# A two-layer hybrid trunk on one core: background products paced by counted TensorE work, sparse values prepared apart, latent queries projected first

## The chip, the cores and the metric

The kernel runs on one core of a Trainium2 chip. The metric is the device time of one execution in microseconds, the median of several runs.

## What is computed

The reference is a decoder trunk of two layers, 512 tokens of width 1024, in float32. A layer normalises its input, projects it at once for four groups of four heads, lets each group attend causally, joins the outputs in one projection that is added to the input, and runs a squared-ReLU MLP of width 4096.

```python
h = rms_norm(x, norm1[l]); proj = h @ w_in[l]
qa = rms_norm(a_cq, mla_q_norm[l]) @ mla_w_uq[l]      # a: latent attention, last 32 of a query's 96 rotated
kv = rms_norm(a_ckv, mla_kv_norm[l]) @ mla_w_ukv[l]
o_a = causal_block_attention(q_a, k_a, kv[..., 64:], 96 ** -0.5)
o_b = sliding_window_attention(q_b, k_b, v_b, sinks[l], Dh ** -0.5)
o_c = dsa_attention(q_c, k_c, v_c, qi, ki, c_w, 128, Dh ** -0.5)   # each query keeps its 128 best keys
o_d = causal_block_attention(..., log_f_cum=cumsum(log_sigmoid(d_f + b)))
x = x + concat(o_a, o_b, o_c, o_d) @ w_out[l]
x = x + square(relu(rms_norm(x, norm2[l]) @ w_up[l])) @ w_down[l]
```

## The kernel before, in words

**Arithmetic.** Every float32 operand of a product is split into a high part (`hi`, a rounding copy, L123 to L127) and a low part (`lo`, the difference, L133 and L135), and a product is three matmuls (`mm3`, L138 to L140): high by high, low by high, high by low. Weights arrive by DMA in `raw` tiles of 512 KB; ScalarE writes the high part `wh`, VectorE or POOL the low part `wl`.

**Stages of a layer.** First comes the projection for the indexer and its scores. Then all other input projections stand in a queue of generators: a, b0, b, d0, d, dv, c0, c, cv, then the four parts o0 to o3 of the output projection over the six head pairs that are ready first. Each step of a generator is one background product, one `mm3` of 128 x 256 (L138 to L140 with `wh` and `T`). After the latent projections (a), the kernel turns them, projects keys and values and then queries from them (four token tiles each), and rotates the queries tile by tile with four operations on POOL (`rotate`, L461 to L466). `prep_a` transposes the rotated queries (L843), then splits them and issues single moves from SP (`move`, L481) that put high and low parts of two heads into stacked tiles `stk`.

**Attention units.** 64 units follow in `run_units`: 16 latent (a), 16 window (b), 16 forgetting (d), 16 sparse (c). A unit is one head's block of 128 queries: score (for d L948 to L950, for c L884 to L893), softmax (VectorE's maximum L538, ScalarE's exponential L541, VectorE's reciprocal L542, POOL's normalisation L546), two units later the transposes of the probabilities and their split (`p_parts`, L552), another two later the product with the values (L595 to L599, L1000 and L1003). Every eight units a new pair of heads begins; its preparation (`prep_b`, `prep_d`, `prep_c`) transposes its rows (`parts`, L487), splits them and moves them through SP. `FIRST` gives the unit from which a preparation may start and `LAG` how many units its projection must have been done. The sparse preparation needs both "c" (keys) and "cv" (values).

**What sets the order.** At each site of the program `fill(kind)` takes as many products from the queue as the next digit of that kind's string says: `u0`, `u1`, `u2` are the three sites of a unit. The selection of the sparse keys is done in 51 VectorE steps (L759 search, L760 replacement, L763) that `extra` issues after the units at the rate `selr`, one rate for each 16 units. An output part starts when a pair's `mixed` rows are four units old (`mlag`); its last products are added to the residual tile T by VectorE (L446). All SP issues stand in one in-order queue, weight loads (L217) and moves alike.

```python
            def fill(kind):
                n = Q.get(kind, "")
                j = site.get(kind, 0)
                site[kind] = j + 1
                for _ in range(int(n[j], 36) if j < len(n) else 0):
                    if not queue or not advance():
                        break
```

## Time and profile before

| | |
|---|---|
| median of 3 runs | 1339.31 us (1338.87 to 1339.56) |
| profiled execution, its own time | 1341.57 us |
| its span | 1339.8 us |
| mean granted TensorE clock | 0.983 |
| busy: TensorE, VectorE, ScalarE, POOL | 1266.1, 733.0, 568.3, 271.4 us |
| DMA | 136.79 MB, mean 102 GB/s |

A time is in microseconds from the start of the span. A line is that of the kernel before. Matmuls overlap: each shows about 0.28 us for 256 columns, though the next one starts earlier, so the time of a run of matmuls is the distance of their starts. The granted clock of 1.00 is 2.4 GHz, 0.5 is 1.2 GHz; a stretch shows its mean. Idle time of an engine is put down to what ended it, and "issue" means that nothing in the profile shows it. In layer 0 attention lies between about 100 and 305 us, in layer 1 between 760 and 965.

### The profile page before, as it was taken

How to read it: one execution, taken by the hardware profiler on the slowest of the kernel's cores; microseconds unless marked ns; L12 is line 12 of the kernel's file. 1: busy time of each engine (PE TensorE's matmuls, PEld its weight loads, DVE VectorE, ACT ScalarE, POOL GpSimd, SP SyncE). 2: the span in 40 equal slices, each digit the busy share in tenths (PEclk: the TensorE clock that was granted, in tenths of full speed). 3: DMA queues.
4: the chain of work that ended last, by engine and by line, in shares of the span. 5: the costliest groups of instructions: out<-in, count | busy, mean ns of one | idle time of the engine just before them, and what ended most of it. 6: DMA issues, size and time to landing. Idle time of an engine off the chain costs nothing.

```text
span 1339.8 us, 19388 instructions
## 1 busy us (share of the span) xinstructions
PE 1266.1 (95%) x7226; PEld 1106.7 (83%) x7232; DVE 733.0 (55%) x1523; ACT 568.3 (42%) x1159; POOL 271.4 (20%) x390
## 2 busy tenths in 40 slices
PE   8889989799999999999989899897999999999997
PEld 7779988698888888888888799887888888888885
DVE  4748989745453334433366498895454523344344
ACT  5745556643442113332337455574344411233231
POOL 3453346331000000000024632642400000000011
PEclk9989999899999999999999999998999999999998
DMA  5135426422333333334412443353333333333331
GB/s 179 48 105 156 106 77 158 102 78 74 110 95 94 98 104 94 97 95 126 138 61 73 118 122 107 91 139 80 105 93 95 95 95 99 96 103 96 110 111 63
DMA packets 50818, 136.79 MB, mean 102 GB/s; under 512 B 7460, under 2 KB 7716, under 8 KB 50724
## 3 DMA queue, kind: packets, MB, share of 16 engines
q1 hardware_dynamic: 50724, 135.55, 35.2%
q8 instruction: 57, 0.93, 0.3%
q14 instruction: 37, 0.30, 0.1%
HBM read 106.95 MB, written 4.19 MB: 83 GB/s over the span
## 4 chain that ended last, share of the span: by engine, by line
PE 79%; DVE 11%; ACT 3%; POOL 3%; issue 2%; DMA 1%; SPq 0%; POOLq 0%; ACTq 0%; DVEq 0%
PE bank L138 24%; PE bank L139 23%; PE bank L140 23%; PE bank L552 2%; DVE wl L133 1%; DVE m L759 1%; DVE mn L538 1%; DMA stk<-prt 1%; DVE isc L760 1%; DVE prt L133 1%; PE bank L597 1%; ACT y L125 1%; PE bank L248 1%; POOL y L465 1%; DVE pt1l L133 1%
## 5 line engine op out<-in xcount | busy, mean ns | idle before, releaser
L123 ACT ACTIVATE wh<-raw 128x1024 fp32r<-128x1024 f32 (+2 forms) x196 | 199.4, 1020 | 286.4 <-PE bank L139 246.5
L133 DVE TENSOR_TENSOR wl<-raw,wh 128x1024 fp32r<-128x1024 f32 (+2 forms) x154 | 188.8, 1228 | 229.6 <-ACT wh L123 229.2
L138 PE MATMUL bank<-wh,T 128*128 128x256 f32 (+3 forms) x864 | 272.6, 316 | 13.7 <-DVE T L446 8.4
L140 PE MATMUL bank<-wl,T 128*128 128x256 f32 (+3 forms) x864 | 257.9, 299 | 1.3 <-DVE wl L133 0.9
L139 PE MATMUL bank<-wh,T 128*128 128x256 f32 (+3 forms) x864 | 257.3, 298 | 0.2 <-DVE T L135 0.2
L140 PE MATMUL bank<-T,wh 128*128 128x512 f32 x512 | 199.5, 390 | 1.0 <-DVE T L135 1.0
L138 PE MATMUL bank<-T,wh 128*128 128x512 f32 x512 | 199.8, 390 | 0.0
L138 PE MATMUL bank<-wh,gh 128*128 128x512 f32 x512 | 199.6, 390 | 0.0
L139 PE MATMUL bank<-T,wl 128*128 128x512 f32 x512 | 199.5, 390 | 0.0
L140 PE MATMUL bank<-wl,gh 128*128 128x512 f32 x512 | 199.2, 389 | 0.0
L139 PE MATMUL bank<-wh,gl 128*128 128x512 f32 x512 | 199.2, 389 | 0.0
L138 PEld LDWEIGHTS bank<-wh,T 128*128 128x128 f32 x864 | 168.8, 195 | 18.7 <-DVE T L446 6.8
L133 POOL TENSOR_TENSOR wl<-raw,wh 128x1024 fp32r<-128x1024 f32 (+3 forms) x42 | 88.2, 2100 | 447.6 <-DVE wl L133 336.5
L140 PEld LDWEIGHTS bank<-wl,T 128*128 128x128 f32 x864 | 168.2, 195 | 4.3 <-DVE wl L133 1.8
L139 PEld LDWEIGHTS bank<-wh,T 128*128 128x128 f32 x864 | 168.9, 196 | 3.2 <-DVE T L135 0.5
L1111 DVE TENSOR_TENSOR a<-a 128x512 f32<-128x512 f32 x64 | 44.3, 693 | 154.1 <-ACT a L1110 154.1
L1110 ACT ACTIVATE a<-bank 128x512 f32<-128x512 f32 x64 | 38.3, 598 | 201.2 <-PE bank L140 201.2
L140 PEld LDWEIGHTS bank<-T,wh 128*128 128x128 f32 x512 | 96.1, 188 | 21.9 <-DVE T L135 1.8
L139 PEld LDWEIGHTS bank<-T,wl 128*128 128x128 f32 x512 | 96.1, 188 | 20.5 <-DVE wl L133 0.7
L138 PEld LDWEIGHTS bank<-T,wh 128*128 128x128 f32 x512 | 96.1, 188 | 20.0 <-ACT T L252 0.3
L138 PEld LDWEIGHTS bank<-wh,gh 128*128 128x128 f32 x512 | 96.1, 188 | 20.0
L546 POOL TENSOR_SCALAR pr<-pr,sm 128x256 f32<-128x256 f32 (+3 forms) x128 | 72.9, 570 | 195.9 <-DVE sm L542 166.9
(209 smaller groups left out, 1852.8 us busy)
## 6 DMA issues: line engine op xcount, KB each, us to landing
raw<-in_wu_dram SPq DMA_DIRECT2D x64, 512.0 KB, 3.6
raw<-in_wd_dram SPq DMA_DIRECT2D x64, 512.0 KB, 3.6
stk<-prt SPq DMA_DIRECT2D x144, 128.0 KB, 2.4
raw<-in_ww_dram SPq DMA_DIRECT2D x32, 512.0 KB, 3.6
T<-in_x_dram SPq DMA_DIRECT2D x16, 256.0 KB, 4.5
raw<-in_wo_dram SPq DMA_DIRECT2D x8, 512.0 KB, 3.6
raw<-in_wa_dram SPq DMA_DIRECT2D x8, 416.0 KB, 3.4
raw<-in_wi_dram SPq DMA_DIRECT2D x8, 300.0 KB, 3.4
```

Of the source, the lines that this page charges most:

```text
L123: S.activation(out=out, in_=in_, func=AF.Copy)
L125: S.activation(out=out, in_=in_, func=AF.Copy, scale=scale)
L133: eng.tensor_tensor(out=out, in0=in_, in1=f(h), op=OP.subtract)
L138: T.matmul(out, ah, bh, start=start, stop=False)
L139: T.matmul(out, al, bh, start=False, stop=False)
L140: T.matmul(out, ah, bl, start=False, stop=stop)
L248: T.transpose(self.ps[k][:, t * P:(t + 1) * P], xs[t][c][:, kk * P:(kk + 1) * P], idf)
L465: eng.tensor_tensor(out=xv, in0=xv, in1=cos[:, None, :].to_broadcast([P, n, w]), op=OP.mult)
L546: NE.tensor_scalar(out=pr[:, 0:ncopy], in0=pr[:, 0:ncopy], scalar1=sm, scalar2=1.0, op0=OP.mult, op1=OP.mult)
L552: T.transpose(ps[:, b * P:(b + 1) * P], pr[:, b * P:(b + 1) * P], idf)
L1110: S.activation(out=a, in_=ps, func=AF.Relu)
L1111: V.tensor_tensor(out=a, in0=a, in1=a, op=OP.mult)
```

## The change

- `pace` replaces the three strings of digits: a counter `spent` adds up TensorE's time by formulas (scores, transposes, value products, `parts`, and 0.36 us for a product), and at the two sites of unit i products are taken until the counter is at (i + 0.5) x 2.75 and (i + 1) x 2.75 us; it may lag by at most five products. The site after the value products is gone, and the preparations' own fills, except that of the first.
- The sparse preparation is split: keys and queries (`c0`, `c1`) need only "c", start at units 41 and 48 instead of 43 and 50 with lag 4 instead of 8; the values (`c0v`, `c1v`) are a step of their own six units later, or when the first value product needs them.
- Latent queries are projected ahead of keys and values, their latent rows turned first, and rotated on VectorE instead of POOL.
- The selection's rates become 1.1, 1.2, 1.1, 1.2 steps per unit (before 1.6, 1.0, 1.0, 1.2).
- The rows of the forget gates (`lf`) take a tile of the pool of two that serves the turned rotated queries, when they are prepared, and `st` has ten buffers instead of nine.

```diff
-    "u0": "14316104302351230042353030803038122120222050241004050962042240222002",
-    "u1": "11343530333211324331352260124662222212120b01002200000102503121410200",
-    "u2": "0000200020000010002000011010000000000000000000002140010010000000000h",
...
-    "hold": ['g', 'b1'], "q3": "VGV", "high": 200, "gate_b": 0, "gate_d0": -1, "lag_b": 6, "lag_c": 8,
-    "steps": 2, "mlag": 4, "first": [0, 11, 18, 21, 26, 33, 43, 50], "psa": 2, "pss": 2, "pst": 3,
+    "hold": ['g', 'b1'], "q3": "VGV", "high": 200, "gate_b": 0, "gate_d0": -1, "lag_b": 6, "lag_c": 4,
+    "steps": 2, "pace": 2750, "quantum": 360, "burst": 5, "mlag": 4, "first": [0, 11, 18, 21, 26, 33, 41, 48], "psa": 2, "pss": 2, "pst": 3,
...
-    "wlo0": "GGVV", "wlo1": "GVGV", "wlop": "GGGG", "selr": [1.6, 1.0, 1.0, 1.2], "tlag": 2,
+    "wlo0": "GGVV", "wlo1": "GVGV", "wlop": "GGGG", "selr": [1.1, 1.2, 1.1, 1.2], "tlag": 2,
...
-            st = pool("st", 9)
+            st = pool("st", 10)
...
+            def pace(until):
+
+                spent[0] = max(spent[0], until - PRM["burst"] * PRM["quantum"])
+                while spent[0] < until and queue and advance():
+                    spent[0] += PRM["quantum"]
...
                         u["score"](ps)
+                        spent[0] += u["ns"]
...
-                    fill("u0")
+                    pace((i + 0.5) * PRM["pace"])
...
+                        spent[0] += 108 * u["nb"] + 82
+                    pace((i + 1) * PRM["pace"])
                     if i >= pl and units[i - pl]["post"]:
                         units[i - pl]["post"]()
-                    fill("u2")
+                        spent[0] += units[i - pl]["pv"]
                     prepare(steps)
...
-                    fill(name)
+                    if at[0] < 0 or name == "a0":
+                        fill(name)
...
-            for j in (2, 0, 1):
+            for j in range(3):
...
-                mm3(ps, cth[2][:, c], ctl[2][:, c], wkv[:, 0], wkv[:, 1], True, True)
-                hi(ykn[:, t], ps[:, 0:256], S, r2[:, 4 + t:5 + t])
-                hi(ykv[:, t], ps[:, 256:512], S, r2[:, 4 + t:5 + t])
-                fill("up")
-            for t in range(NT):
-                ps = bank("s")
-                c = slice(t * P, (t + 1) * P)
                 for j in range(2):
                     mm3(ps[:, 0:384], cth[j][:, c], ctl[j][:, c], wq_h[:, j * 384:(j + 1) * 384],
                         wq_l[:, j * 384:(j + 1) * 384], j == 0, j == 1)
                 hi(yqr[:, t, 0:128], ps[:, 256:384], S, r2[:, t:t + 1])
                 hi(yqn[:, t], ps[:, 0:256], S, r2[:, t:t + 1])
-                rotate(yqr[:, t, 0:128], 4, 16, t)
+                rotate(yqr[:, t, 0:128], 4, 16, t, V)
+                fill("up")
+            for t in range(NT):
+                ps = bank("s")
+                c = slice(t * P, (t + 1) * P)
+                mm3(ps, cth[2][:, c], ctl[2][:, c], wkv[:, 0], wkv[:, 1], True, True)
+                hi(ykn[:, t], ps[:, 0:256], S, r2[:, 4 + t:5 + t])
+                hi(ykv[:, t], ps[:, 256:512], S, r2[:, 4 + t:5 + t])
                 fill("up")
...
-            lf = ix.tile([P, 512], F32, tag="lf", name="lf")
             def prep_gates0():
+                lf = gate["f"] = kl_p.tile([P, 512], F32, tag="kl", name="lf")
                 G.memset(lf, 0.0)
...
                 def prep_c(o=o, p=p):
-                    yield from pair_64(o, ys["c0"], ys["c"], ys["cv"], 128 * p)
-                preps.append((f"c{p}", FIRST[6 + p], ("c", "cv"), prep_c()))
-                units += causal_units(f"c{p}", score_c, o, 4 + p)
+                    yield from pair_64(o, ys["c0"], ys["c"], 128 * p)
+
+                def prep_cv(o=o, p=p):
+                    o["vs"] = v_pair(heads(ys["cv"], 128 * p))
+                    yield
+                preps.append((f"c{p}", FIRST[6 + p], ("c",), prep_c()))
+                preps.append((f"c{p}v", FIRST[6 + p] + 6, ("cv",), prep_cv()))
+                units += causal_units(f"c{p}", score_c, o, 4 + p, lambda n: 3 * (n + 32) / 2.4)
```

The order of instructions moves at three places that matter here. The line numbers of the changed kernel differ: its `mm3` is L127 to L129.

TensorE ahead of the transposes of layer 0's rotated latent queries (L843 before, L844 in the change, on `y`); matmuls of 128x384 from `stk` project the queries, those of 128x512 keys and values, those of 128x256 are background products. Before:

```order
L138 MATMUL bank<-stk,T 128x384
L139 MATMUL bank<-stk,T 128x384
L140 MATMUL bank<-stk,T 128x384
L138 MATMUL bank<-wh,T 128x256
L139 MATMUL bank<-wh,T 128x256
L140 MATMUL bank<-wl,T 128x256
L138 MATMUL bank<-wh,T 128x256
L139 MATMUL bank<-wh,T 128x256
L140 MATMUL bank<-wl,T 128x256
L843 MATMUL bank<-idf,y 128x128 x4
L487 MATMUL bank<-idf,y 128x128 x4
```

In the change:

```order
L127 MATMUL bank<-stk,T 128x512
L128 MATMUL bank<-stk,T 128x512
L129 MATMUL bank<-stk,T 128x512
L127 MATMUL bank<-wh,T 128x256
L128 MATMUL bank<-wh,T 128x256
L129 MATMUL bank<-wl,T 128x256
L127 MATMUL bank<-wh,T 128x256
L128 MATMUL bank<-wh,T 128x256
L129 MATMUL bank<-wl,T 128x256
L844 MATMUL bank<-idf,y 128x128 x4
L484 MATMUL bank<-idf,y 128x128 x4
```

The matmuls in front are now those of keys and values; the queries' own stand further ahead.

TensorE at the start of layer 0's second pair of forgetting heads (score: before L948 to L950, in the change L949 to L951; `pr` are the probabilities, transposed at L552 and L548). Before:

```order
L948 MATMUL bank<-stk 128x256
L949 LDWEIGHTS idb
L949 MATMUL bank<-masks,idb 128x128
L950 MATMUL bank<-gk_84,stk 128x256
L552 MATMUL bank<-idf,pr 128x128 x3
L948 MATMUL bank<-stk 128x256
L949 LDWEIGHTS idb
L949 MATMUL bank<-masks,idb 128x128
L950 MATMUL bank<-gk_84,stk 128x256
L552 MATMUL bank<-idf,pr 128x128 x4
L595 MATMUL bank<-pt0h_396,stk 128x256
```

In the change:

```order
L949 MATMUL bank<-stk 128x256
L950 LDWEIGHTS idb
L950 MATMUL bank<-masks,idb 128x128
L951 MATMUL bank<-gk_84,stk 128x256
L127 MATMUL bank<-wh,T 128x256
L128 MATMUL bank<-wh,T 128x256
L129 MATMUL bank<-wl,T 128x256
L548 MATMUL bank<-idf,pr 128x128 x3
L127 MATMUL bank<-wh,T 128x256
L128 MATMUL bank<-wh,T 128x256
L129 MATMUL bank<-wl,T 128x256
L127 MATMUL bank<-wh,T 128x256
```

Between a score and the transposes, where nothing stood, there are now products.

VectorE where the first output part of layer 0 is added to T (L446 before, L443 in the change; `stk<-y,stk` is the low part of the sparse values, `mn` and `sm` belong to the softmax). Before:

```order
L127 CAST stk<-y 128x8x64
L446 TENSOR_TENSOR T<-bank,T 128x256
L542 RECIPROCAL sm<-sm 128x1
L133 TENSOR_TENSOR stk<-y,stk 128x8x64
L567 TENSOR_TENSOR tmp<-bank,tmp 64x512
L538 TENSOR_REDUCE mn<-bank 128x1
L133 TENSOR_TENSOR pt1l_401<-bank,pt1h_397 128x3x128
L446 TENSOR_TENSOR T<-bank,T 128x256
L542 RECIPROCAL sm<-sm 128x1
L446 TENSOR_TENSOR T<-bank,T 128x256 x2
```

In the change:

```order
L122 TENSOR_TENSOR pt1l_393<-bank,pt1h_389 128x3x128
L122 TENSOR_TENSOR T<-tmp,T 128x512
L538 RECIPROCAL sm<-sm 128x1
L122 TENSOR_TENSOR pt1l_393<-bank,pt1h_389 128x4x128
L534 TENSOR_REDUCE mn<-bank 128x1
L122 TENSOR_TENSOR pt0l_400<-bank,pt0h_396 128x128
L534 TENSOR_REDUCE mn<-bank 128x1
L538 RECIPROCAL sm<-sm 128x1
L443 TENSOR_TENSOR T<-bank,T 128x256 x3
L538 RECIPROCAL sm<-sm 128x1
L443 TENSOR_TENSOR T<-bank,T 128x256
```

The values' split has moved ahead of the adds, and the adds stand closer together.

## Rows read from the trace of the kernel before

**Rows 1.** The page: TensorE's busy time (share, instructions), and the shares of the engines in the chain that ended last.

```profile
PE 1266.1 (95%) x7226; PEld 1106.7 (83%) x7232; DVE 733.0 (55%) x1523; ACT 568.3 (42%) x1159; POOL 271.4 (20%) x390
PE 79%; DVE 11%; ACT 3%; POOL 3%; issue 2%; DMA 1%; SPq 0%; POOLq 0%; ACTq 0%; DVEq 0%
```

**Rows 2.** The timeline around 262.8 us, TensorE alone: two consecutive matmuls of one background product (start, duration, engine, line, operation, operands).

```profile
262.80 0.28 PE L138 MATMUL bank<-wh,T 128*128 128x256 f32 x1
262.92 0.28 PE L139 MATMUL bank<-wh,T 128*128 128x256 f32 x1
```

**Rows 3.** A table of stretches of 20 us: the stretch, its length, then busy time (and instructions) of TensorE, of its weight loads, of VectorE, ScalarE and POOL, the granted TensorE clock, the share of the DMA engines and GB/s.

```profile
80.00:100.00 20.00, 14.87 (x98) 14.26 (x97) 6.62 (x10) 6.43 (x13) 13.37 (x24) 0.83 0.30 66
140.00:160.00 20.00, 20.00 (x168) 19.30 (x167) 19.78 (x56) 12.36 (x32) 5.73 (x8) 1.00 0.43 110
160.00:180.00 20.00, 18.51 (x158) 18.06 (x156) 16.02 (x37) 9.92 (x26) 4.49 (x6) 1.00 0.30 90
180.00:200.00 20.00, 17.57 (x145) 16.85 (x146) 15.91 (x49) 12.43 (x31) 12.08 (x16) 1.00 0.26 70
200.00:220.00 20.00, 19.95 (x168) 19.27 (x167) 18.18 (x50) 11.85 (x33) 14.42 (x19) 1.00 0.60 161
220.00:240.00 20.00, 17.82 (x139) 15.79 (x138) 19.15 (x53) 14.28 (x39) 8.63 (x13) 1.00 0.58 137
240.00:260.00 20.00, 14.32 (x89) 12.21 (x89) 13.31 (x35) 10.59 (x30) 4.25 (x8) 0.83 0.39 86
260.00:280.00 20.00, 17.48 (x127) 16.22 (x126) 11.28 (x30) 9.73 (x26) 6.69 (x9) 0.91 0.25 64
360.00:380.00 20.00, 20.00 (x90) 16.57 (x89) 8.58 (x11) 9.96 (x19) 0.00 (x0) 1.00 0.36 105
740.00:760.00 20.00, 14.67 (x106) 14.25 (x105) 6.64 (x10) 7.58 (x15) 14.50 (x28) 0.91 0.30 67
900.00:920.00 20.00, 14.19 (x92) 12.06 (x93) 13.99 (x36) 11.37 (x34) 4.36 (x9) 0.91 0.43 95
920.00:940.00 20.00, 17.48 (x128) 16.38 (x128) 11.17 (x31) 9.41 (x26) 7.33 (x9) 0.91 0.20 51
```

**Rows 4.** The list of TensorE's waits over the whole span: waiting line and what ended the wait, us in total, times, longest.

```profile
PE bank L843 <- POOL y L466: 10.3, 4, 4.0
PE bank L138 <- DVE T L446: 8.4, 8, 2.5
PE bank L884 <- issue: 4.4, 1, 4.4
```

**Rows 5.** The preparation of layer 0's first heads: POOL's first operation of one tile's rotation undisturbed and beside a weight split on VectorE (timeline, in order of time), and the group of POOL's last rotation operation on 128 columns by shape (count | busy us, mean ns | idle before).

```profile
79.46 0.32 POOL L461 TENSOR_TENSOR tmp<-y,rope 128x64 f32<-128x64 f32 x1
83.33 1.62 DVE L133 TENSOR_TENSOR wl<-raw,wh 128x1024 fp32r<-128x1024 f32 x1 [0.84 <-ACT wh L123]
83.83 1.30 POOL L461 TENSOR_TENSOR tmp<-y,rope 128x64 f32<-128x64 f32 x1
...
L466 POOL TENSOR_TENSOR y<-y,tmp 128x128 f32<-128x128 f32 x14 | 6.3, 456 | 0.6
```

**Rows 6.** The same place in layer 1: the eviction that follows the query transposes, the moves that SP issues, and the second matmul of the first attention unit.

```profile
750.26 0.60 ACT L123 ACTIVATE kst<-bank 128x512 fp32r<-128x512 f32 x1 [4.64 <-PE bank L843]
750.89 2.53 SPq L481 DMA_DIRECT2D stk<-kst  x4
...
753.51 7.59 SPq L481 DMA_DIRECT2D stk<-prt  x12
...
761.00 0.39 PE L879 MATMUL bank<-stk 128*128 128x256 f32 x1
```

**Rows 7.** Around the first sparse unit of layer 0: SP issues two weight loads, ScalarE evicts the last transposes of its rows, SP issues moves of it, TensorE starts its first score.

```profile
228.80 5.27 SPq L217 DMA_DIRECT2D raw<-in_wo_dram  x2
243.93 0.60 ACT L123 ACTIVATE prt<-bank 128x512 fp32r<-128x512 f32 x1
246.39 10.61 SPq L481 DMA_DIRECT2D stk<-prt  x5
248.80 0.56 PE L884 MATMUL bank<-stk 128*128 128x256 f32 x1 [4.25 <-DMA stk<-prt]
```

**Rows 8.** VectorE's groups by shape: the search of the eight largest over 512 keys.

```profile
L759 DVE MAX8 m<-isc 128x8 f32<-128x512 f32 x32 | 21.8, 681 | 0.0
```

**Rows 9.** POOL's normalisations of 128 columns: one beside a weight split, one later, and all of this shape.

```profile
189.35 1.86 POOL L546 TENSOR_SCALAR pr<-pr,sm 128x128 f32<-128x128 f32 x1 [2.89 <-DVE sm L542]
267.53 0.37 POOL L546 TENSOR_SCALAR pr<-pr,sm 128x128 f32<-128x128 f32 x1 [1.20 <-DVE sm L542]
...
L546 POOL TENSOR_SCALAR pr<-pr,sm 128x128 f32<-128x128 f32 x32 | 16.3, 509 | 57.8 <-DVE sm L542 47.1 <-PE bank L949 6.4 <-PE bank L552 4.3
```

**Rows 10.** The start of the second output part in layer 0: the low part of the values, one of the adds to T, and the first product behind them.

```profile
264.65 1.13 DVE L133 TENSOR_TENSOR stk<-y,stk 128x512 fp32r<-128x512 f32 x1
266.96 0.41 DVE L446 TENSOR_TENSOR T<-bank,T 128x256 f32<-128x256 f32 x1
267.42 0.39 PE L138 MATMUL bank<-wh,T 128*128 128x256 f32 x1 [2.52 <-DVE T L446]
```

**Rows 11.** POOL's group of the zeroing of the gate rows.

```profile
L899 POOL MEMSET lf<- 128x512 f32 x2 | 1.1, 537 | 0.0
```

More of the change, by code (lines that the diff above doesn't have):

```diff
@@ L39 @@
     "a0": "cc0",
-    "u0": "14316104302351230042353030803038122120222050241004050962042240222002",
-    "u1": "11343530333211324331352260124662222212120b01002200000102503121410200",
-    "u2": "0000200020000010002000011010000000000000000000002140010010000000000h",
-    "a1": "120",
-    "b0": "0020",
-    "b1": "10",
-    "g": "08",
-    "d0": "000",
-    "d1": "001",
-    "c0": "0920",
-    "c1": "0500",
     "aq": "603",
@@ L382, in fill @@
                         break
+            spent = [0.0]
+            def pace(until):
+                spent[0] = max(spent[0], until - PRM["burst"] * PRM["quantum"])
+                while spent[0] < until and queue and advance():
+                    spent[0] += PRM["quantum"]
             def upto(name):
@@ L487, in parts @@
                     T.transpose(ps[:, t * P:(t + 1) * P], y[:, t, c0:c0 + P], idf)
+                spent[0] += 514
                 h_, l_ = part_tile(), part_tile()
@@ L520, in v_pair, with pair_64 @@
                 return d
-            def pair_64(o, yq, yk, yv, c0):
+            def pair_64(o, yq, yk, c0):
                 o["ks"] = stack()
@@ L528, in pair_64 @@
                 q_rows(o["qs"], *parts(yq, c0))
-                yield
-                o["vs"] = v_pair(heads(yv, c0))
                 yield
@@ L574, in finish_head, with causal_units @@
                     mixed_at[st_["k"]] = at[0] + PRM["mlag"]
-            def causal_units(need, score, o, k):
+            def causal_units(need, score, o, k, cost):
                 st_ = {"k": k}
@@ L591, in post @@
                                 hst["pv"] = bank("v")
+                            if "vs" not in o:
+                                prepared(need + "v")
                             pv, vs = hst["pv"], o["vs"]
@@ L604, in causal_units @@
                             need=need, score=lambda ps, h=h, qb=qb, n=max(256, nv): score(o, ps, h, qb, n), nv=nv, nc=nv,
-                            nb=qb + 1, dh=ph_[:, 0:qb + 1, q0:q0 + P], dl=pl_[:, 0:qb + 1, q0:q0 + P],
+                            ns=cost(max(256, nv)), pv=480 * (half + 1), nb=qb + 1, dh=ph_[:, 0:qb + 1, q0:q0 + P], dl=pl_[:, 0:qb + 1, q0:q0 + P],
                             post=post if qb % 2 else None))
@@ L925, in prep_gates @@
                 for t in range(NT):
-                    T.transpose(ps[:, t * P:(t + 1) * P], lf[:, t * P:(t + 1) * P], idf)
+                    T.transpose(ps[:, t * P:(t + 1) * P], gate["f"][:, t * P:(t + 1) * P], idf)
                 cum = temp()
@@ L1006, in post @@
                             finish_head(pv, h, st_)
-                        out.append(dict(need=need, score=score, nv=nk + 2, nc=nk, nb=nk // P, dh=dv(ph_), dl=dv(pl_),
+                        out.append(dict(need=need, score=score, nv=nk + 2, nc=nk, ns=360, pv=960, nb=nk // P, dh=dv(ph_), dl=dv(pl_),
                                         post=post if qb == 3 else None))
@@ L1016, in tile_trunk @@
                 preps.append((f"a{p}", FIRST[0], (), prep_a(o, p)))
-                units += causal_units(f"a{p}", score_a, o, p)
+                units += causal_units(f"a{p}", score_a, o, p, lambda n: 3 * (n + 32) / 2.4 + 67)
             for g in range(2):
@@ L1041, in tile_trunk @@
                 preps.append((f"d{p}", FIRST[4 + p], ("d", "dv"), prep_d()))
-                units += causal_units(f"d{p}", score_d, o, 6 + p)
+                units += causal_units(f"d{p}", score_d, o, 6 + p, lambda n: 2 * (n + 32) / 2.4 + 67)
             for p in range(2):
```

1 line of the change is left out of this document (removed).

## The prediction

> **What bounds the kernel.** I read the busy shares first, then TensorE's waits, then a table of stretches, then the single rows of each stall. TensorE is busy for 1266.1 of 1339.8 us and makes 79% of the chain that ended last [rows 1]: the span is the time in which TensorE issues its matmuls, plus its holes. A background product's matmuls follow each other by 0.12 us [rows 2], so a product of three costs 0.36 us wherever it stands. The MLP has no holes (20.00 of 20 us, clock 1.00, 90 matmuls of 512 columns, so 0.22 us each [rows 3]) and the change does not touch it. What it can win are the holes of attention, which the list of waits names [rows 4]: the transposes of the latent queries behind POOL's rotation (10.3 us in 4 waits), the first sparse score of a layer behind its moves (4.4, shown as issue; in the other layer 4.25, as a single row below shows), products behind VectorE's adds to T (8.4). Some are followed by a granted clock of 0.83 or 0.91 over 20 us [rows 3]; at half rate that is (1 - 0.83) x 20 = 3.4 us lost, or 1.8.
>
> The profiled execution took 1341.57 us; the median of the runs is 2.3 us less, and I take this off at the end. The change adds no matmul and no transfer: the gain can only be holes, and the order of work decides.
>
> **Term 1, queries first.** Today the last matmuls ahead of the query transposes (L843) are the query projection's own, then two products; the rotation on POOL (about 0.32 us twice and 0.46 twice a tile [rows 5]) is also held up: one 0.32 us operation took 1.30 beside a VectorE split that began 0.5 us earlier [rows 5]. In the new order four latent triples (12 x 0.22) and six products (6 x 0.36) stand between, 4.8 us; the last tile's rotation needs an eviction and four short operations, 2 to 3 us even at POOL's rates. So the 10.3 us go, and with them the slow clock after: 3.4 us in layer 0, 1.8 in layer 1 [rows 3]. Together 15.5. But a new wait is behind it. The 4 + 12 moves of the first heads go out through SP one by one, some 0.63 us each, from 0.63 us after the transposes; the second matmul of the first unit ran 10.74 us after them (750.26 to 761.00) and still waited for its DMA [rows 6]. TensorE filled those 10.7 us partly at half clock; without about 1 us of that it is there after 9.3. I charge 1.4 to 1.5 us a layer, 3.0 in all. **Net 12.5.** Bounds: 15.5 (no wait) and 8 (SP takes 2 us longer each time).
>
> **Term 2, sparse keys early.** The first sparse score waits 4.4 and 4.25 us [rows 4, 7], 8.7 in all, since its last part is evicted at 243.93 and SP issues the moves from 246.39; TensorE starts at 248.80 [rows 7]. After it the clock costs 3.4 and 1.8 us. Together 13.9. The preparation no longer needs the values and starts two units earlier with half the lag; counted in the new order, its first transposes stand 16.8 us of TensorE work before that score (6.1 before). Today's chain from the second eviction to the score is 4.9 us, so the added lead of 10.7 us covers it twice. I keep 0.9 for small slips. **Net 13.0**; bounds 13.9, and 0 if the moves stand behind a blocked weight load again: at 228.80 two such loads held SP for 5.27 us [rows 7].
>
> **Term 3, products spread.** Window and forgetting units now hold five or so products each; before, most of the last forgetting units had none, so a softmax chain had nothing beside it. TensorE's idle time in 160:180, 180:200 and 220:240 is 1.49, 2.43 and 2.18 us [rows 3], 6.1 a layer. Not all of it goes, because VectorE is nearly full: in 140:240 it is busy 89.0 us of TensorE's 93.9 [rows 3]. The lower selection rate for the first units moves some eight selection steps from the latent units into these, a search of 0.68 us at full width [rows 8] and a replacement that I count alike, less for narrow blocks: about 8 us more, so 97 against 94. In 140:160 VectorE was busy 19.78 with TensorE at 20.00 [rows 3], so a full VectorE need not stall TensorE, but an overrun of 3 us must be paid. I keep 3 us a layer. **Net 6**; bounds 12 and minus 11 (all of it at the pace of 220:240, first rival).
>
> Here a rule speaks against the change. What the rows show: a normalisation on POOL took 1.86 us, where another of its shape took 0.37, while VectorE split a weight; but the 32 of this shape average 0.509, so such meetings are few [rows 9]. The Trainium skill, page "SBUF — State Buffer", section "SBUF: two separate sides", says that a VectorE instruction with two SBUF inputs and a GpSimd instruction that reads SBUF exclude each other for a whole instruction. By the rows I keep 3 us a layer and the sum below is 1304; by that rule, with VectorE full of splits and rotations, the first rival's 1321 would come out. The 1.86 and the 1.30 us rows agree with it, their rarity so far with the sum.
>
> **Term 4, the first product of the second output part.** It waits 2.52 us for VectorE's adds to T, which stand behind a value split of 1.13 us and others [rows 10], and the clock falls after it (1.8 [rows 3]): 4.3 a layer, 8.6. In the new order the value split is gone from between the adds, but the same adds (four of some 0.41) directly precede the product, with 12 matmuls, 1.44 us, as cover, and by the new order VectorE has 8.8 us of work (rows by shape) against 5.2 of TensorE in those units. Half remains. **Net 3.6**; bounds 8.6 and 0.
>
> **Priced at nothing.** The later zeroing of the gate rows is 0.54 us of POOL [rows 11] ahead of the third unit's normalisation; a softmax result is used two units (5 us) later, which covers it. A tenth st buffer costs nothing. If that cover fails, each is under 1 us.
>
> **Sum:** 12.5 + 13.0 + 6 + 3.6 = 35.1; 1341.57 - 35.1 - 2.3 = 1304.
>
> **Rivals.** *VectorE becomes the limit of the window and forgetting units, and POOL with it.* For it: 97 against 94 us above, and the normalisation that a weight split held for 1.5 us [rows 9]. Against it: 140:160 and the mean of 0.509. Price: 93.9 us of work at 17.82 per 20 loses 11.5 us a layer where 6.1 are lost now, so minus 10.8 in place of plus 6: gain 18.3, time 1321.
>
> *The two late stalls only move.* Terms 2 and 4 fail, through SP's queue and VectorE's order: gain 18.5, time 1321. For it: SP's 10.61 us for five moves [rows 7]; against it: the 10.7 us of added lead.
>
> *Slower: SP's in-order queue misses the starts of groups.* Products that come later free weight buffers later; a weight load that waits for its buffer holds every move behind it, as the 5.27 us at 228.80 do. Each group of four heads' moves that comes late then costs what the sparse one costs now, 4.3 us and 1.8 of clock, 6.1. There are 14 group starts after the first units; six misses eat the 35 us, eight give 1304 + 49 = 1353. For it: by my count of the new order the window heads' moves land less than 1 us ahead of need. Against it: all others have about 5 us, and each group has 21 us for some 18 moves of 0.63.
>
> *It does not do what it says:* the counted costs could space the products as the table did. The order of instructions says otherwise (the forgetting units differ), so little is left to this: 1339.
>
> **Numbers.** Forecast 0.58, VectorE 0.16, stalls move 0.14, slower 0.08, no change 0.04. A measurement of this kernel tells apart about 0.2%, 2.7 us. Faster 0.88, same 0.04, slower 0.08. The low end is all of the four terms, 15.5 + 13.9 + 12.2 + 8.6 = 50.2, so 1289; the high end takes in both milder rivals, 1323. Most of the chance lies with one sign.
>
> **What would show it.** Right: no wait at the query transposes and clock 1.00 through the preparation, one DMA wait of 1 to 2 us at the first unit, no wait at the first sparse score, TensorE's idle time from the window units to the last forgetting unit about half of today's, VectorE above 95% there. Wrong: waits of several us at starts of groups (SP), or many waits of 0.3 to 1 us on softmax results in the window and forgetting units (VectorE).

## The result and the profile after

The changed kernel takes 1326.31 us (median of four, 1323.49 to 1327.58), the kernel before 1339.43 on the same chip: a ratio of 0.9899 (95% interval 0.9881 to 0.9916). It is faster, as forecast, but by 13.1 us and not by 35; 1326 lies above the range. The profiled execution took 1326.81 us, its span 1324.7 (1339.8 before). In the changed kernel's rows `mm3` is L127 to L129, an eviction L114, a high part L112, a low part L122.

First the page (busy times; the chain that ended last), which answers to [rows 1], and the list of TensorE's waits, which answers to [rows 4].

```profile
PE 1263.0 (95%) x7226; PEld 1102.6 (83%) x7232; DVE 756.5 (57%) x1555; ACT 565.9 (43%) x1159; POOL 263.2 (20%) x358
PE 76%; DVE 12%; ACT 5%; POOL 3%; DMA 2%; issue 2%; SPq 1%; POOLq 0%; ACTq 0%; DVEq 0%
```
```profile
PE bank L127 <- ACT y L114: 13.8, 14, 2.0
PE bank L127 <- DVE T L443: 8.2, 6, 2.2
...
PE bank L548 <- POOL pr L542: 4.3, 7, 0.9
...
PE bank L484 <- DVE y L463: 2.0, 2, 1.0
```

The same wait for an eviction (`y` from a bank), as the list of before has it:

```profile
PE bank L138 <- ACT y L125: 5.1, 6, 1.5
```

The 10.3 us at the query transposes and the 8.7 us at the first sparse scores are gone. On top are now waits of a product for ScalarE's eviction: 14 of 13.8 us in all, where there were 6 of 5.1; the waits for adds to T are as long in total as before. The chain has less TensorE, more VectorE and ScalarE in it.

The table of stretches, with the columns of [rows 3]:

```profile
80.00:100.00 20.00, 18.01 (x128) 17.02 (x127) 8.59 (x17) 8.79 (x19) 10.97 (x14) 0.92 0.52 128
140.00:160.00 20.00, 17.91 (x151) 17.25 (x150) 19.20 (x57) 11.89 (x32) 4.20 (x8) 1.00 0.33 90
160.00:180.00 20.00, 18.00 (x141) 17.50 (x141) 18.42 (x46) 11.95 (x31) 5.00 (x8) 0.91 0.17 54
180.00:200.00 20.00, 19.14 (x163) 18.61 (x161) 19.88 (x56) 10.95 (x32) 11.68 (x15) 1.00 0.59 145
200.00:220.00 20.00, 18.28 (x146) 16.96 (x144) 18.04 (x49) 12.39 (x32) 14.41 (x20) 1.00 0.54 121
220.00:240.00 20.00, 17.09 (x136) 15.71 (x135) 19.18 (x49) 11.00 (x28) 8.47 (x9) 1.00 0.55 146
240.00:260.00 20.00, 17.75 (x134) 15.49 (x135) 14.83 (x39) 13.11 (x35) 9.00 (x12) 1.00 0.42 104
300.00:320.00 20.00, 18.12 (x82) 14.64 (x83) 12.43 (x19) 4.82 (x7) 2.52 (x2) 0.91 0.37 105
740.00:760.00 20.00, 18.20 (x144) 16.75 (x142) 13.29 (x38) 8.98 (x22) 12.62 (x22) 1.00 0.84 198
900.00:920.00 20.00, 17.74 (x134) 15.70 (x134) 12.39 (x33) 11.06 (x30) 7.63 (x11) 1.00 0.31 81
```

Against [rows 3] (layer 1 now stands some 15 us earlier), TensorE has fewer idle microseconds in 80:100 and 240:260, 740:760 and 900:920, but more in 140:160 (2.09 where there were none), 160:180, 200:220 and 220:240, and the clock falls in 160:180, where it was whole, and in 300:320. VectorE is busy 94.7 of 100 us from 140 to 240.

A table by stretches of the program says where the 15 us between the two spans came from. "Third unit" is the start of its score, "48th unit" that of the last forgetting unit. "Lost" is the time between two starts in the trace, less the matmuls between them at their distances at full clock (0.12 us for 256 columns, 0.174 for 384, 0.19 for 416, 0.227 for 512, 0.108 for a transpose).

| from | to | lost before, layers 0 / 1 | lost after | difference, both | forecast |
|---|---|---|---|---|---|
| latent projections | third unit | 10.5 / 8.5 | 4.5 / 2.1 | -12.4 | -12.5 (term 1) |
| third unit | 48th unit | 7.4 / 7.3 | 12.9 / 13.1 | +11.3 | -6 (term 3) |
| 48th unit | 53rd unit | 7.4 / 6.6 | -0.1 / -0.1 | -14.2 | -13 (term 2) |
| 53rd unit | 61st unit | 5.2 / 5.2 | 3.3 / 3.4 | -3.7 | -3.6 (term 4) |
| 61st unit | MLP | 3.4 / 3.8 | 7.0 / 7.3 | +7.0 | none |
| all else | | | | -2.7 | none |

Of the last line 3.4 us are a stretch at half clock in layer 1's indexer, which the trace of before shows at 697.9 and that of after does not.

**Term 1 as it came.** SP's issues, the eviction behind the query transposes and the first unit's first two matmuls in layer 0, which answer to [rows 6]:

```profile
85.02 0.60 ACT L112 ACTIVATE kst<-bank 128x512 fp32r<-128x512 f32 x1
85.64 2.52 SPq L478 DMA_DIRECT2D stk<-kst  x4
88.27 8.12 SPq L478 DMA_DIRECT2D stk<-prt  x12
95.67 0.36 PE L879 MATMUL bank<-stk 128*128 128x256 f32 x1 [1.19 <-DMA stk<-prt]
96.47 0.36 PE L880 MATMUL bank<-stk 128*128 128x256 f32 x1 [0.44 <-DMA stk<-prt]
```

From the transposes to the first two matmuls 10.7 and 11.5 us pass, and TensorE waits 1.19 and 0.44 us (1.03 and 0.32 in layer 1): the charge of 1.5 a layer. What was not charged is the half clock that follows in layer 0 (0.92 in 80:100, so 1.6 us lost).

**The boundary.** TensorE's last product of a projection, then VectorE, ScalarE and the next projection's first product at the layer-0 gate preparation (start, duration, engine, operation; in brackets the idle time before and what ended it):

```profile
166.04 0.28 PE L129 MATMUL bank<-wl,T 128*128 128x256 f32 x1
166.55 0.41 DVE L534 TENSOR_REDUCE mn<-bank 128x1 f32<-128x258 f32 x1
167.06 0.48 ACT L537 ACTIVATE pr<-bank,mn 128x258 f32<-128x258 f32 x1 [1.16 <-DVE mn L534]
...
167.79 1.21 ACT L114 ACTIVATE y<-bank,y 128x256 f32<-128x256 f32 x3
168.31 0.39 PE L127 MATMUL bank<-wh,T 128*128 128x256 f32 x1 [2.00 <-ACT y L114]
```

The bank is full at about 166.3. ScalarE stands idle for 1.16 us, since the next instruction in its queue is an exponential that waits for VectorE's maximum; the eviction stands behind it (for the last 0.7 us of that with its bank full), and the product waits 2.00 us. Half clock follows.

**POOL's hold.** The end of attention in layer 0, and a rotation among the forgetting units. Each fence shows POOL's weight split first, then VectorE, then TensorE's wait.

```profile
297.67 2.38 POOL L122 TENSOR_TENSOR wl<-raw,wh 128x1024 fp32r<-128x1024 f32 x1 [6.82 <-ACT wh L112]
298.14 2.45 DVE L122 TENSOR_TENSOR T<-tmp,T 128x512 fp32r<-128x512 f32 x1 [0.79 <-ACT T L112]
300.52 1.40 DVE L443 TENSOR_TENSOR T<-bank,T 128x256 f32<-128x256 f32 x4
301.41 0.53 PE L127 MATMUL bank<-wh,T 128*128 128x512 f32 x1 [2.16 <-DVE T L443]
```
```profile
221.85 2.54 POOL L122 TENSOR_TENSOR wl<-raw,wh 128x1024 fp32r<-128x1024 f32 x1
222.34 2.33 DVE L463 TENSOR_TENSOR y<-y,tmp 128x256 f32<-128x256 f32 x1
224.73 0.87 PE L484 MATMUL bank<-idf,y 128*128 128x128 f32 x6 [1.02 <-DVE y L463]
```

Operations that take 0.68 (134.79, below) and 0.41 us elsewhere end only 0.3 to 0.5 us behind POOL's split. The first holds the adds to T and so the last two output weights' first product by 2.16 us, the second the transposes of a rotated row by 1.02.

```profile
134.79 0.68 DVE L122 TENSOR_TENSOR T<-tmp,T 128x512 fp32r<-128x512 f32 x1
159.27 2.39 POOL L122 TENSOR_TENSOR wl<-raw,wh 128x1024 fp32r<-128x1024 f32 x1 [0.18 <-ACT wh L112]
160.25 1.96 DVE L122 TENSOR_TENSOR T<-tmp,T 128x512 fp32r<-128x512 f32 x1
```

The same operation at 160.25 takes 1.28 us more than at 134.79. From there to 168 VectorE has no idle time, so the maximum at 166.55, for which the boundary above waited, is late by that much.

Over attention in layer 0, VectorE's operations were longer than the lower quartile of their shape by 10.0 us in sum (counting those over by 0.15 and more); 8.2 of it are five operations beside POOL's weight splits (at 114.14, 136.85, 160.25, 222.34 and 298.14). Before the change the sum was 2 to 3 us, as the operations are grouped, and 0.8 of it stood beside such splits.

### The profile page after: what moved, and what is told of

Read it like the earlier page. It is cut to its first block, busy times and chain, and to the rows that moved or that the text cites. A ratio compares the mean times of both kernels' runs of the same rounds, so it can differ in the third digit from the quotient of the medians.

```text
span 1324.7 us, 19396 instructions
## 1 busy us (share of the span) xinstructions
PE 1263.0 (95%) x7226; PEld 1102.6 (83%) x7232; DVE 756.5 (57%) x1555; ACT 565.9 (43%) x1159; POOL 263.2 (20%) x358
## 4 chain that ended last, share of the span: by engine, by line
PE 76%; DVE 12%; ACT 5%; POOL 3%; DMA 2%; issue 2%; SPq 1%; POOLq 0%; ACTq 0%; DVEq 0%
PE bank L127 23%; PE bank L129 22%; PE bank L128 22%; ACT y L114 2%; PE bank L548 1%; DVE isc L761 1%; DVE m L760 1%; DVE mn L534 1%; DVE T L122 1%; PE bank L595 1%; DVE pt1l L122 1%; DMA stk<-prt 1%; SPq L478 1%; DVE wl L122 1%; ACT pr L537 1%
## 5 line engine op out<-in xcount | busy, mean ns | idle before, releaser
L122 DVE TENSOR_TENSOR wl<-raw,wh 128x1024 fp32r<-128x1024 f32 (+2 forms) x154 | 188.2, 1224 | 227.5 <-ACT wh L112 226.8
L112 ACT ACTIVATE wh<-raw 128x1024 fp32r<-128x1024 f32 (+2 forms) x196 | 199.4, 1020 | 267.1 <-PE bank L128 230.2
L127 PE MATMUL bank<-wh,T 128*128 128x256 f32 (+3 forms) x864 | 274.6, 318 | 22.9 <-ACT y L114 13.8
L129 PE MATMUL bank<-wl,T 128*128 128x256 f32 (+3 forms) x864 | 256.4, 297 | 0.9 <-POOL wl L122 0.9
L129 PE MATMUL bank<-T,wh 128*128 128x512 f32 x512 | 199.5, 390 | 0.9 <-DVE T L124 0.9
L127 PE MATMUL bank<-T,wh 128*128 128x512 f32 x512 | 199.8, 390 | 0.0
L127 PE MATMUL bank<-wh,gh 128*128 128x512 f32 x512 | 199.5, 390 | 0.0
L129 PE MATMUL bank<-wl,gh 128*128 128x512 f32 x512 | 199.2, 389 | 0.0
L127 PEld LDWEIGHTS bank<-wh,T 128*128 128x128 f32 x864 | 166.9, 193 | 31.1 <-ACT y L114 17.9
L122 POOL TENSOR_TENSOR wl<-raw,wh 128x1024 fp32r<-128x1024 f32 (+3 forms) x42 | 89.7, 2135 | 429.0 <-DVE wl L122 339.8
L128 PEld LDWEIGHTS bank<-wh,T 128*128 128x128 f32 x864 | 166.9, 193 | 3.6 <-DVE T L124 0.5
L129 PEld LDWEIGHTS bank<-wl,T 128*128 128x128 f32 x864 | 166.3, 192 | 3.2 <-POOL wl L122 1.3
L129 PEld LDWEIGHTS bank<-T,wh 128*128 128x128 f32 x512 | 96.1, 188 | 22.0 <-DVE T L124 1.8
L127 PEld LDWEIGHTS bank<-wh,gh 128*128 128x128 f32 x512 | 96.1, 188 | 19.9
L128 PEld LDWEIGHTS bank<-wh,gl 128*128 128x128 f32 x512 | 96.1, 188 | 19.9
```

What stands on the lines that cost most here:

```text
L112: S.activation(out=out, in_=in_, func=AF.Copy)
L122: eng.tensor_tensor(out=out, in0=in_, in1=f(h), op=OP.subtract)
L127: T.matmul(out, ah, bh, start=start, stop=False)
L128: T.matmul(out, al, bh, start=False, stop=False)
L129: T.matmul(out, ah, bl, start=False, stop=stop)
```

## Experiments

The theories: **boundary** (paced products run across the end of a projection into an eviction), **VectorE's load**, and, from the rows above, **POOL's hold on VectorE**. All medians are of four or more runs, in four groups; the kernel before took 1337.8 to 1339.1 us beside them. The changed kernel's 1326.31 was measured beside a 1339.43, so a difference to it across groups is good to 1 or 2 us, and a trace is that of one execution. "Lost" in a layer moves by 1.7 us with each stretch of 3.4 us at half clock that falls into it.

**Pause at boundaries.**

```diff
-                while spent[0] < until and queue and advance():
+                n = len(done)
+                while spent[0] < until and queue and len(done) == n and advance():
```

> The changed kernel, but the pacing loop stops for the rest of its site when a projection or an output part ends, so that something else of the unit stands between the last product of one and the first of the next. Theory 1, the boundary (paced products run straight across the end of a projection, and the first product of the next waits for ScalarE to evict the bank): the 13.8 us that products wait for evictions in the changed kernel fall to less than half, the 2.0 us ones with their half clock go; 1314 to 1321 us. Theory 2, VectorE is the limit of the window and forgetting units: the holes only move to softmax results, 1324 to 1329 us.

1316.37 us, ratio to before 0.983 (0.9812 to 0.9847), 10 below the changed kernel. TensorE's waits:

```profile
PE bank L127 <- DVE T L444: 9.8, 10, 2.2
PE bank L127 <- ACT y L114: 8.1, 14, 1.6
...
PE bank L129 <- DVE wl L122: 5.3, 2, 2.7
```

The time is the boundary theory's; the list is not. The eviction waits fall only from 13.8 to 8.1, and a wait for VectorE's weight split, 2.7 us in each layer, is new. From the third to the 48th unit 11.3 and 9.8 us are still lost (12.9 and 13.1 in the changed kernel); the other half of the gain is half clock that is missing at the starts and ends of attention.

**The selection's rates of before** (`selr` 1.6, 1.0, 1.0, 1.2).

> The changed kernel with the selection's rates of before (1.6, 1.0, 1.0, 1.2). Theory 1 (boundary): no difference beyond 2 us, 1324 to 1328. Theory 2 (VectorE the limit): eight selection steps, about 8 us of VectorE a layer, leave the window and forgetting units, and up to 5 us a layer come back: 1316 to 1321.

1323.78, ratio 0.9889 (0.9874 to 0.9903): 2.5 less, between the two, and the runs of the two kernels overlap (1322.46 to 1323.88 against 1323.49 to 1327.58). The waits on evictions are 9.4 us and VectorE's excess is 5.1 us a layer (10.0 in the changed kernel), but the first window scores now wait for their moves, 3.9 and 3.6 us:

```profile
PE bank L127 <- ACT y L114: 9.4, 12, 1.6
...
PE bank L988 <- DMA stk<-prt: 3.9, 1, 3.9
PE bank L988 <- issue: 3.6, 1, 3.6
```

This is the place where the prediction's slower rival counted less than 1 us to spare.

**The digits of before in place of the pacing** (`fill("u0")`, `fill("u1")`, `fill("u2")` and the preparations' fills; the rest of the change kept).

> The changed kernel with the three strings of digits and the preparations' fills of before in place of the pacing; all else of the change is kept. Theory 1: the pacing itself loses some 5 us a layer between the first window and the last forgetting unit by boundaries and 3.5 us at the end of attention, so without it the kernel is faster than the changed one unless the sparse rows come late again: 1310 to 1318. Theory 2: the stalls of the last forgetting units come back and VectorE's load is the same, 1324 to 1332.

1334.48, ratio 0.9967 (0.9955 to 0.9979). The boundary theory's figure was wrong: the pacing is worth 8 us; the other theory's range is missed too, by 2.5. The trace shows where most of it lies:

```profile
PE bank L896 <- DMA stk<-prt: 3.8, 1, 3.8
PE bank L896 <- issue: 3.7, 1, 3.7
```

The first sparse scores wait again, since with these digits "c" is projected later: in this order the rows' transposes stand 8.5 us of TensorE work ahead of the score, in the changed kernel 16.8. Term 2 needs the pacing. The same trace limits what the pacing can be blamed for: from the third to the 48th unit 10.5 and 11.7 us are lost (7.4 before, 12.9 and 13.1 in the changed kernel), although VectorE's excess is only 2.5 us a layer. In this order most of the loss is there without the pacing and without POOL's hold.

**Keys and values first** (order and POOL's rotation of before).

> The changed kernel with keys and values projected ahead of the queries again, the latent rows turned in the old sequence and the rotation on POOL: that one part undone. If the two preparations together are worth the 11.4 us that the excess of the span over the matmuls' own time shows (4.5 and 6.9), 1336 to 1339 us; if the faster preparation is mostly given back at the first unit's wait, 1328 to 1332.

1334.81, ratio 0.9974 (0.9964 to 0.9985): 8.5 us more than the changed kernel, between the two expectations; the waits at the transposes are back in full.

```profile
PE bank L844 <- POOL y L463: 10.2, 4, 4.0
```

**The sparse preparation undone.**

```diff
-                preps.append((f"c{p}", FIRST[6 + p], ("c",), prep_c()))
+                preps.append((f"c{p}", FIRST[6 + p], ("c", "cv"), prep_c()))
...
```

The part left out puts lag 8, units 43 and 50, and the values' step back to the same unit.

> The changed kernel with the sparse preparation as before: keys and queries need the values' projection too, lag 8, units 43 and 50. Its first transposes then stand 5.8 us of TensorE work ahead of the first sparse score (16.8 in the changed kernel, 6.1 before). If the split of the preparation is what removed the sparse wait, 4 us and some half clock come back in each layer: 1334 to 1339 us. If the pacing removed it by spreading the load, 1325 to 1329 us.

1339.60, ratio 1.0009 (0.9993 to 1.0024): 13.3 us come back, in sum the size of term 2. The trace, that of the fastest of ten runs, has 8.8 us more than the changed kernel's: 5.3 at the sparse units, 4.7 at the output parts behind them and 3.8 ahead of them, less what other places gain. So term 2's own place accounts for less than half. The early preparation and the pacing each are needed.

```profile
PE bank L885 <- DMA stk<-prt: 5.0, 2, 2.6
```

**Three banks for products, two for transposes** (`"psa": 3, "pst": 2`).

> The changed kernel with three banks for the background products and two for the transposes (two and three before). Theory 1 (a paced product that starts the next projection waits for the eviction of its bank): two products, 0.72 us, are gained at each boundary, so the waits on evictions fall by more than half, 1316 to 1322 us. Theory 2 (VectorE and ScalarE are late as such): the holes move to the transposes, which now have a bank less; 1325 to 1335 us.

1321.14, ratio 0.9867 (0.9844 to 0.989). No wait on an eviction is left among the longer ones, but others took their place:

```profile
PE bank L548 <- DVE prt L122: 7.3, 6, 1.9
PE bank L548 <- POOL pr L542: 7.3, 10, 1.8
```

From the third to the 48th unit 12.4 us are lost in layer 0, 10.7 in layer 1. This points to the boundary as the place where lateness shows, not where it comes from.

**Half of the selection left out.**

> The changed kernel with half of the selection steps left out: only the 64 best keys are searched, so some 24 steps, about 25 us of VectorE a layer, are missing from the 24th unit on. Theory 2 (VectorE the limit): the losses between the 24th and the 48th unit, 6.5 us a layer in the changed kernel, fall below 2: 1315 to 1319 us. Theory 1: the eviction waits stay, 1322 to 1326 us.

1317.27, ratio 0.9839 (0.9822 to 0.9857). In the second half of the stretch (25th to 49th unit) 3.2 and 3.5 us are lost in place of 6.5: half, not nearly all. VectorE's load counts.

**POOL standing still at the end of attention.**

> The kernel with the pause at boundaries (1316 us), in which the low part of the last two output weights is not computed on POOL but zeroed by ScalarE, so that POOL stands still at the end of attention. In the changed kernel VectorE's split of the last mixed rows took 2.45 us at 298.14 where 0.72 is usual, while POOL split a weight (297.67 to 300.05). If POOL holds VectorE there, the split is back at 0.7 us, the 2.2 us wait of the first product behind it falls to about 0.5 in both layers: 1311 to 1314 us. If the products' order itself is at fault (too few products cover the adds), the wait stays: 1315 to 1317 us.

1313.02, ratio 0.981 (0.9788 to 0.9832), 3.4 below the pause alone; the two intervals overlap, and the rows decide: from the 61st unit to the MLP 3.5 us a layer are lost in place of 5.2. The same place: ScalarE's write in place of the weight split, VectorE's split, and the product:

```profile
292.31 1.05 ACT L178 ACTIVATE wl<-raw 128x1024 fp32r<-128x1024 f32 x1
292.44 0.69 DVE L122 TENSOR_TENSOR T<-tmp,T 128x512 fp32r<-128x512 f32 x1 [0.79 <-ACT T L112]
293.94 0.47 PE L127 MATMUL bank<-wh,T 128*128 128x512 f32 x1 [0.40 <-DVE T L447]
```

0.69 for 2.45 us, and a wait of 0.40 for 2.16: the hold is what the 2 us were.

**Evictions ahead of the softmax on ScalarE.**

```diff
-                    hi(y, ps, S, scale[:, t:t + 1])
+                    with tc.high_priority(offset=400):
+                        hi(y, ps, S, scale[:, t:t + 1])
```

> The changed kernel with the evictions of the background projections given more priority than the softmax, so that on ScalarE they stand ahead of the next exponential; no product moves. If ScalarE's in-order queue makes the boundary wait (at 166.04 the eviction stood behind an exponential that waited 1.2 us for VectorE's maximum), the waits on evictions fall from 13.8 to under 6 us: 1317 to 1321 us. If the wait is just the time that an eviction takes, nothing changes: 1324 to 1328.

1320.95, ratio 0.9864 (0.9846 to 0.9882): 5.4 less. So, in the changed kernel, ScalarE's queue did make part of the wait; the rest moved:

```profile
PE bank L548 <- POOL pr L542: 8.4, 7, 2.3
...
PE bank L129 <- DVE wl L122: 5.9, 2, 3.0
PE bank L127 <- ACT y L114: 4.8, 10, 0.9
```

**Pause and half selection together.**

> The pause at boundaries together with half of the selection steps left out. Each alone took about 9 to 10 us off the changed kernel. If boundary and VectorE's load are two separate causes, the gains add: 1306 to 1309 us. If they are one chain (VectorE's late maximum holds ScalarE's exponential, and the eviction that the next projection waits for stands behind it), each already takes most of it: 1312 to 1316 us.

1314.67, ratio 0.9817 (0.9777 to 0.9856): by the median the gains do not add, though the four runs lie 10 us apart (1308.79 to 1319.10).

**Pause, evictions first, end weights on VectorE:**

> A version meant to be kept: the pause at boundaries, evictions ahead of the softmax on ScalarE, and the last two output weights split on VectorE instead of POOL. If the causes are the boundary and POOL's hold on VectorE: 1308 to 1313 us. If VectorE's load decides, the added split at the end and the moved evictions give nothing more than the pause: 1315 to 1318 us.

1316.16, ratio 0.9824 (0.98 to 0.9847), no better than the pause alone. Against the last version below, which lacks only the moved evictions (1310.72), evictions first gain nothing beside the pause.

**POOL reads nothing.**

```diff
-                split_weight(w_raw[j], n, h[:, 0:n], l[:, 0:n], eng)
+                if eng is G:
+                    hi(h[:, 0:n], w_raw[j][:, 0:n], S)
+                    G.memset(f(l[:, 0:n]), 0.0)
+                    G.memset(f(l[:, 0:n]), 0.0)
+                else:
+                    split_weight(w_raw[j], n, h[:, 0:n], l[:, 0:n], eng)
```

> The changed kernel with POOL's share of the weights' low parts not computed: POOL zeroes those tiles twice instead, which keeps it as long but reads nothing. VectorE's operations were longer than usual by some 10 us a layer in attention (3 before the change), while POOL split weights. If POOL's reading holds VectorE, these 10 us vanish, the 2.45 us split at the end is 0.7 again, and the kernel is at 1312 to 1319 us. If only POOL's occupation counts, 1323 to 1328.

1311.96, ratio 0.9797 (0.9779 to 0.9816), 14.3 below the changed kernel. VectorE at the end of attention, and POOL's two zeroings beside it:

```profile
292.10 0.95 POOL L196 MEMSET wl<- 128x1024 f32 x1
292.80 0.69 DVE L122 TENSOR_TENSOR T<-tmp,T 128x512 fp32r<-128x512 f32 x1 [0.78 <-ACT T L112]
```

At the boundary of 166.04 the same split of mixed rows, and the product that waited 2.00 us:

```profile
159.60 0.68 DVE L122 TENSOR_TENSOR T<-tmp,T 128x512 fp32r<-128x512 f32 x1
166.40 0.39 PE L127 MATMUL bank<-wh,T 128*128 128x256 f32 x1 [0.73 <-ACT y L114]
```

The split is 1.28 us shorter and the wait 1.27, and no half clock follows: this link of the chain is shown. The other waits on evictions mostly stay: 10.3 us in 12 waits are left of 13.8 in 14. The mean granted clock of the profiled execution is 0.994 against 0.989, which by the difference in clock times the span, an estimate, is some 6.7 us of the gain.

VectorE's excess falls to 2 to 3 us a layer; from the third to the 48th unit 8.1 us are lost in both layers (12.9 and 13.1 with the reading). The zeroings differ in two more ways: they take 1.9 us in place of 2.4 and need not wait for the high part.

**The same in the kernel before.**

> The kernel before, with POOL's share of the weights' low parts zeroed instead of computed. If the hold is made worse by the change (10 us a layer against 3), this gains at most a third of the 14 us that it gains in the changed kernel: 1333 to 1337 us. If it was there as much before: 1324 to 1328.

1335.72, ratio 0.998 (0.997 to 0.9991): 2 us. The hold, and the zeroings' other two differences, cost little there; in the order of the change they are dear.

**The hold away and the pause; the hold away and half the selection.**

> POOL zeroes its share of the weights' low parts twice instead of computing them (it reads nothing), and the pacing pauses at boundaries. If the eviction waits are the end of one chain that begins with POOL holding VectorE, the pause adds little to the 1312 us: 1308 to 1312. If the boundary is a cause of its own, its 10 us come off as well: 1301 to 1305.

1312.63, ratio 0.981 (0.9795 to 0.9824): in time the pause adds nothing once POOL does not hold VectorE. That does not show one chain, for the clock differs: it is 0.990 here and 0.994 without the pause, about 5 us (an estimate, the difference in clock times the span). From the third to the 48th unit 7.9 and 8.1 us are lost, and each holds a stretch at half clock (at 196.5 and 838.2) that the kernel without the pause does not have there; at full clock some 6.3 would be lost in place of its 8.1. Waits on evictions fall from 10.3 to 5.0 us, and 5.4 for VectorE's weight split are new. So the traces leave room for the boundary as a cause of its own, whose gain the clock takes back; one chain is not shown.

> POOL's low parts zeroed as above, and half of the selection steps left out. If VectorE's own load matters beside POOL's hold, the 8 us a layer that remain between the third and the 48th unit fall below 5: 1304 to 1308. If the hold alone made VectorE late: 1310 to 1313.

1305.91, ratio 0.9757 (0.9743 to 0.9772): VectorE's load adds 6 us. From the third to the 48th unit 6.1 us a layer are lost, less than 8.1 but not the "below 5" expected.

**A version to keep: the pause, and the last two output weights split on VectorE.**

```diff
-        wlist += [(wt_d[L, c], 1024, G, "") for c in range(2)]
+        wlist += [(wt_d[L, c], 1024, V, "") for c in range(2)]
```

> The pause at boundaries, and the last two output weights split on VectorE instead of POOL; the whole computation is kept. VectorE's split of the mixed rows is no longer held for 1.8 us, but its own weight split of 1.25 us may stand ahead of the adds: gain over the pause alone (1316) between 0 and 3.5 us, 1312 to 1316.

1310.72, ratio 0.98 (0.9782 to 0.9819): the whole computation, 15.6 us below the changed kernel and the fastest of those that leave nothing out. The two ranges do not touch (1308.31 to 1312.61 against 1323.49 to 1327.58). It is 5.6 below the pause alone, more than expected. Of this 1.8 lies at the end of attention, where the edit acts (4.3 us a layer lost in place of 5.2); some 4 us are clock (0.995 against 0.992), since the half clock that the pause alone shows at 145.0, 196.2 and 841.3 is missing, though the edit changes nothing there. Why is open.

## Why the prediction was wrong

**What bounds the kernel**: right. The holes decided, and the four terms sit where they were placed.

**Terms 1, 2 and 4**: right in place and size, 12.4, 14.2 and 3.7 us in the table against 12.5, 13.0 and 3.6. Undone alone, term 1 is worth 8.5 and term 2 13.3. Three details differ. Term 4's figure does not follow from its working ("half" of 8.6 is 4.3, not 3.6), so that its match is in part luck. Term 2 was put down to the early preparation; the runs show that it needs the pacing as much, which brings "c" forward. Term 4's wait fell from 2.52 to 0.64 us, more than forecast, but two softmax waits of 0.6 to 0.8 us beside it were not foreseen.

**Term 3 is the step that failed**: "Net 6" became minus 11.3, at the lower bound that it named ("minus 11"). The prediction kept 3 us a layer because a full VectorE had not stalled TensorE in 140:160 and because the POOL operations that a VectorE split held were few. It priced only what VectorE does to POOL. What the trace shows most plainly is the other direction: POOL's 2.4 us splits held VectorE's operations (8.2 of the 10.0 us by which they were longer in layer 0, before 0.8 of 2 to 3), on an engine that had 97 us of work for 94 to begin with (measured: busy 119.9 of the 133.7 us from the third to the 48th unit before, 130.7 of 137.4 after, 124.6 of 132.6 with the zeroings). At one boundary a layer this lateness ran on through ScalarE's queue (exponential ahead of eviction) to the first product of the next projection, 2.00 us and half clock.

The prediction had a row of it in hand: the value split of 1.13 us in [rows 10] took 0.68 us elsewhere, and POOL split a weight beside it, from 263.95 to 265.23. The row was priced as VectorE's work and not as a hold.

Of the 17.3 us by which the term was off, the zeroings, which take the hold away, give back 9.8 (8.1 us a layer lost in place of 12.9 and 13.1). Their shorter time and their freedom from the high part were not separated from the hold; the rows show that the held operations themselves are back at 0.68 us. The other 7.5 are a second failure of the same step: even without the hold the spread products lose 8.1 us a layer, where 7.4 were lost before and 4.4 were forecast. Shown for this part are VectorE's load (half of the selection left out: 6.1 a layer) and the boundary, where 10.3 us of eviction waits remain. Which part of the change loads the stretch, the pacing, the selection's rates or the rotation on VectorE, was not separated, and that is open.

The sign that was named for this, many waits on softmax results, came only in part (4.3 us in 7 waits); most of the loss showed in a place that the prediction did not name, the evictions.

**What had no term** is the end of attention, plus 7.0: the same hold, a wait of 2.16 us in each layer, and the half clock after it. With POOL standing still there the loss is back at 3.5 us a layer, as before the change.

**The rule against the row.** Of the Trainium skill's page "SBUF — State Buffer", section "SBUF: two separate sides", the prediction said that by rows 1304 would come out and by the rule 1321. The rows of after side with the rule (2.45 us for 0.68, ending 0.5 us behind POOL's split), and the time, 1326, is nearer to its figure. The rule names whichever engine starts second as the loser; the prediction used only one half of it.

**The rivals.** The first, VectorE and POOL with it, at 0.16, is what happened, at 1326 where it gave 1321 (the end of attention, plus 7.0, is more than the rest); its evidence beside the 97 against 94 was a normalisation on POOL held by VectorE, the reverse of what cost the time. Stalls that only move did not occur. The slower rival's place, the window heads' rows, showed 3.9 and 3.6 us of wait only when the old selection rates were put back.

## What to carry to other kernels

An order that counts one engine's time can move load onto the engines that were not counted: cost their work over the same stretch, with what holds them, before calling a hole filled. Where two engines exclude each other, look in both directions: the long operation of the idle engine (2.4 us on POOL) holds short ones of the full engine. A wait that disappears when its bank or its place is changed may only be where lateness surfaces; a second remedy that adds nothing to the first in time may cut the same chain, or may pay its gain back in clock: compare what is lost at full clock before calling it one chain.

## What the runs showed of the hardware

VectorE operations of two SBUF operands that began beside POOL's weight split ended 0.3 to 0.5 us behind it, however early they began (0.68 us became 2.45 and 1.96, 0.41 became 2.33); a copy of gate rows was held in the same way (0.15 us became 1.84 at 114.14, ending with the split). Operations with one operand from a bank kept their time beside such splits (0.68 us at 181.21, 0.41 at 271.99). Zeroing on POOL did not hold the subtraction (0.69 us for one that began during a zeroing).

ScalarE idled 1.16 us behind a waiting exponential, the last 0.7 of it while an eviction that was ready stood behind it. A wait of 1.2 us at the first unit was followed by half clock in layer 0, and one of 1.0 in layer 1 was not; with the zeroings one of 1.82 us there was not either.
